# One kernel for a whole transformer layer: no ada rows in the last value group of the first input projection, and 1.06 rows per unit in the first output projection

## The chip, the cores and the metric

The kernel runs on one core of one Trainium2 chip. The metric is the device time of one execution in microseconds (us); for the kernel before the change three runs are given.

## What is computed

One layer over 256 tokens of width 2048, in float32: a first SwiGLU block of inner width 5632, a token mixer (forget-gate attention and an mLSTM), and a second SwiGLU block. Each block takes a layer norm of the running activation, shifted and scaled by values computed from a condition vector `c`, and each block's result is gated by further values of the same kind before it is added back.

```python
def _modulate(x, shift, scale):
    return _layernorm(x) * (1 + scale) + shift

def _swiglu(h, w_in, w_out):
    gate, up = jnp.split(h @ w_in, 2, axis=-1)
    return (jax.nn.silu(gate) * up) @ w_out

...
    ada = (jax.nn.silu(c) @ w_ada + b_ada)[:, None, :]
    sh1, sc1, g1, sh2, sc2, g2, sh3, sc3, g3 = jnp.split(ada, N_ADA, axis=-1)
    h = _swiglu(_modulate(x, sh1, sc1), ffn1_w_in, ffn1_w_out)
    x = _layernorm(ALPHA * x + 0.5 * (1 + g1) * h, ln1_g, ln1_b)
    h = _token_mixer(_modulate(x, sh2, sc2), w_in, fox_f_bias, mlstm_conv_w, mlstm_conv_b,
                     mlstm_i_bias, mlstm_f_bias, mlstm_norm_g, w_out)
    x = _layernorm(ALPHA * x + (1 + g2) * h, ln2_g, ln2_b)
    h = _swiglu(_modulate(x, sh3, sc3), ffn2_w_in, ffn2_w_out)
    x = _layernorm(ALPHA * x + 0.5 * (1 + g3) * h, ln3_g, ln3_b)
```

The product of `c` with `w_ada` (2048 by 18432) is the "ada" work. The change touches only when parts of it are done.

## The kernel before

**Matrix products.** Every large product is made of three TensorE matmuls on split operands: a float32 matrix is split into a rounded part `hi` (a cast on ScalarE, L155) and a remainder `lo` (a subtraction on VectorE, L156), and `hi*hi`, `hi*lo` and `lo*hi` are added up in PSUM (L435 to L437). Weights come by DMA on SyncE's queue into `raw` tiles of 1 MB (three of them), are split in two halves of 128x1024 into `hi` and `lo` tiles (six of each), and are used once. One `raw` tile is called a unit here.

**The first SwiGLU block.** `ffn_in` multiplies by `ffn1_w_in`. Its loop takes 256 inner features at a time, first the gate columns (`gu` = 0) and then the up columns (`gu` = 1, the value group); two PSUM tiles `gu_f` hold both. At the end of each turn ScalarE takes the silu of the gate half into `hT` (L474) and VectorE multiplies it by the up half (L475). `out_proj` then multiplies `hT` by `ffn1_w_out` in columns of 1024, 512 and 512. Its first four PSUM tiles, `o_f`, come from the same rotation of five as `gu_f`: with two tiles held by the last turn, the fourth `o_f` tile is one of those two, and is free when its L475 is done. On L156's tiles the two stages are called `f1i` and `f1o`.

**The ada rows.** A row of ada work is a DMA of 512 KB of `w_ada` into a tile `ar` (two of them, tag `araw`, L188 and L189) and one multiply-and-add on VectorE into an accumulator `acc` (L170). Sixteen rows make one accumulator of the queue; then a tail splits it and sums it over partitions on TensorE (`bc`, L183), with a few small VectorE steps (`dg`, `scsh`, L200 to L204). The rows are handed out along the way by a queue object: after each half unit, and after each unit, the stage's rate is credited and whole rows that are owed are written into the program.

```python
        def half_step(self):
            n = self.rate / 2
            self.given += n
            self.owed += n
            self.owed_rows()

        def pump(self, n):
            self.owed += n - self.given
            self.rate, self.given = n, 0
            self.end_step()
            self.owed_rows()

        def rest(self):
            self.owed = self.rate = self.given = 0
```

The rates stand in one line (L814): 1.2 rows per unit in the first input projection (`R_IN`), 1 in the first output projection (`R_OUT`). `out_proj` pumps after 40 of its 44 units: the last four get tails alone. Before it ends, at `need(6)`, the four accumulators for the mixer's shift and scale (`acc3_0` to `acc3_3`, shown as `acc_0` to `acc_3`) must be complete; the boundary to the mixer reads them.

**What sets the order.** Dependencies are tracked by the framework, which also orders each engine's instructions from the written program; VectorE, ScalarE and SyncE then run their lists strictly in that order.

Of the kernel before, what the change touches and what calls it, by code (L numbers as in the profile page):

```python
# [32 lines left out]
def layer_kernel(  # L33
# [35 lines left out]
    def mm_tile(name, four=False):  # L69
        turn[0] = 0 if four else turn[0] % 5 + 1  # L70
        if turn[0] == 5:
            return fifth_tile(name)
        return pm.tile([P, 512], F32, tag="mm", bufs=4, name=name)
# [218 lines left out]
    ada = AdaQueue()  # L292
# [134 lines left out]
    def unwoven(ps):  # L427
        return ps.rearrange("p (n a) -> p a n", a=2)

    def halves(v):  # L430
        return v.rearrange("p (a n) -> p a n", a=2)

    def mm3(o, ah, al, bh, bl, start, stop):
        bh, bl = woven(bh), woven(bl)
        PE.matmul(o, ah, bh, start=start, stop=False)  # L435
        PE.matmul(o, ah, bl, start=False, stop=False)  # L436
        PE.matmul(o, al, bh, start=False, stop=stop)  # L437

    def mm2(o, ah, al, x, start, stop):
        PE.matmul(o, ah, x.rearrange("p s (a n) -> p s n a", a=2), start=start, stop=False)  # L440
        PE.matmul(o[:, T:], al, woven(x[:, 0]), start=False, stop=stop)  # L441


    def cols_form_a(src, c0, outs, xT, name, npump, khs=(0, 1)):
        xhi, xlo, x = xT
        for kh in khs:
            for k8, hi, lo in load_w(src[kh * 1024:(kh + 1) * 1024, c0:c0 + 256], 8, 256, f"{name}_{kh}"):
                k = kh * 8 + k8
                for f in range(2):
                    fs = slice(f * P, (f + 1) * P)  # L450
                    start, stop = k == 8 * khs[0], k == 8 * khs[-1] + 7
                    if outs[f].shape[-1] == 2 * T:
                        mm2(outs[f], hi[:, fs], lo[:, fs], x[:, k], start, stop)
                    else:
                        mm3(outs[f], hi[:, fs], lo[:, fs], xhi[:, k, :], xlo[:, k, :], start, stop)
            npump()

    def ffn_in(w, xT, hT, j0, tag, npump, values=None):
        def one(j, gu, outs):
            last = gu and j == DFF // 256 - 1  # L460
            cols_form_a(w, gu * DFF + j * 256, outs, xT, f"{tag}i{j}_{gu}", (lambda: None) if last else npump)

        def both(dst, ps):
            S.copy(dst, unwoven(ps[:, :T]))
            V.tensor_tensor(out=dst, in0=dst, in1=unwoven(ps[:, T:]), op=ALU.add)

        for j in range(j0, DFF // 256):
            if values is None:
                ps = [mm_tile(f"gu_{tag}{j}_{f}") for f in range(2)]
                for gu in range(2):  # L470
                    one(j, gu, [p[:, gu * T:(gu + 1) * T] for p in ps])
                for f in range(2):
                    h = halves(hT[:, 2 * j + f, :])
                    S.activation(h, unwoven(ps[f][:, :T]), AF.Silu)  # L474
                    pin["h"] = V.tensor_tensor(out=h, in0=h, in1=unwoven(ps[f][:, T:]), op=ALU.mult).ins  # L475
                continue
            for gu in range(2):
                ps = [mm_tile(f"gu_{tag}{j}_{gu}{f}") for f in range(2)]
                one(j, gu, ps)
                for f in range(2):  # L480
                    h = halves(hT[:, 2 * j + f, :])
                    if gu:
                        u = halves(values.tile([P, T], F32, tag="u", bufs=2, name=f"u_{tag}{j}_{f}"))
                        both(u, ps[f])
                        pin["h"] = V.tensor_tensor(out=h, in0=h, in1=u, op=ALU.mult).ins
                    else:
                        both(h, ps[f])
                        S.activation(h, h, AF.Silu)
        for _ in range(2):
            npump()  # L490


# [312 lines left out]
    def entry_of(load, got, u0, u1):  # L805
        for u in range(u0, u1):
            got[u] = []
            for item in load(u):
                got[u].append(item)
                yield  # L810

    R_F, R_IN, R_OUT, R_MX, R_A, R_B = 1.25, 1.2, 1, 1.26, 1, .7  # L814
    NP = 2
    right = dict(side="right")
    def at(rate):
# [255 lines left out]

    first_hi_places("1")
    ffn_in(W1, xT, hT, NS, "f1", at(R_IN))
    xp.release()
    need(2)
# [62 lines left out]
    fence, _, xs, ws = boundary(*ent["f"], ent["lgb"], 3, "1", xT, entry_of(mo_load, mow, 3, 6), KD, raws)  # L1140
# [14 lines left out]
    xhi, xlo, _ = xT  # L1155
# [522 lines left out]
    for us in (0, 1), (2,):  # L1678
        for q in QS:
            last = q == QS[-1]  # L1680
# [27 lines left out]
    h_parts.clear()  # L1708
    vals = tc.alloc_tile_pool(name="vals2", bufs=1)
    ffn_in(W2, xT, hT, 2 + NH, "f2", at(R_B), vals)  # L1710
    vals.release()
    need(14)
# [42 lines left out]
```

## Time and profile before

| what | us |
|---|---|
| three runs | 1862.06, 1863.48 (median), 1869.91 |
| the profiled execution, its own time | 1865.56 |
| its span in the profile | 1863.9 |
| TensorE matmuls busy in it | 1830.1 |
| VectorE busy | 1455.8 |
| ScalarE busy | 913.5 |

The times are of whole executions; the profile is of one more execution, and the sum in the prediction is made against that one's own time, 1865.56 us. In the rows that follow, PE is TensorE's matmuls, PEld its weight loads, DVE VectorE, ACT ScalarE, SPq SyncE's DMA queue. Times in timelines are counted from the start of the span. A row of a timeline gives the start, the duration of the (merged) instructions, the engine, the line, the operation, what it writes and reads, and, in brackets, how long the engine had been idle and what released it.

### The profile page before, as it was taken

To read this page: it belongs to the slowest core of one execution; us is meant where nothing else is said; L and a number is where in the kernel's file an instruction comes from. 1 tells how busy PE (TensorE), PEld (TensorE's weight loads), DVE (VectorE), ACT (ScalarE), POOL (GpSimd) and SP (SyncE) were. 2 spreads that over 40 slices of the span, in tenths; PEclk is the share of its full clock that TensorE was granted. 3 is DMA by queue.
4 is the path that set the end of the run, shared out by engine and by line. 5 is a ranking of instruction groups with operands and counts; after the bars stand their busy time and mean duration, and the time that the engine had idled before them with its cause. 6 is when DMAs were issued, how large, how long until landed. Compare 5 with 4: busy or idle time off the path is not lost.

```text
span 1863.9 us, 30963 instructions
## 1 busy us (share of the span) xinstructions
PE 1830.1 (98%) x12521; PEld 1694.2 (91%) x12521; DVE 1455.8 (78%) x1819; ACT 913.5 (49%) x1290; POOL 62.1 (3%) x92
## 2 busy tenths in 40 slices
PE   7999999999999999999999999999999999999997
PEld 5999999999988888689999887999999999988887
DVE  6889989778788787778889878777998776574655
ACT  3554454443454434655566645545454444554441
POOL 1211200000000000000000000000000000000000
PEclk9999999999999999999999999999999999999999
DMA  9989978999897889389978883998878876666663
GB/s 366 383 278 316 319 236 283 321 322 318 285 324 273 311 296 326 129 283 330 313 275 293 324 290 131 343 324 271 293 255 275 273 251 201 198 202 204 204 203 144
DMA packets 263431, 510.82 MB, mean 274 GB/s; under 512 B 10834, under 2 KB 93426, under 8 KB 262264
## 3 DMA queue, kind: packets, MB, share of 16 engines
q1 hardware_dynamic: 255176, 477.90, 74.9%
q0 software_dynamic: 8112, 30.95, 4.8%
q8 instruction: 98, 1.61, 0.4%
q14 instruction: 45, 0.37, 0.1%
HBM read 506.71 MB, written 2.10 MB: 273 GB/s over the span
## 4 chain that ended last, share of the span: by engine, by line
PE 56%; DVE 2%; DMA 1%; issue 1%; ACT 0%; POOL 0%; DVEq 0%; ACTq 0%; POOLq 0%
PE gu_f L440 8%; PE o_f L435 4%; PE o_f L437 4%; PE o_f L436 4%; PE fh L435 4%; PE fh L437 4%; PE fh L436 4%; PE gu_f L441 4%; PE o_mx L435 1%; PE o_mx L436 1%; PE o_mx L437 1%; PE b_mv L435 1%; PE pr_m L435 1%; PE b_mv L436 1%; PE b_mv L437 1%; PE pr_m L437 1%
## 5 line engine op out<-in xcount | busy, mean ns | idle before, releaser
L170 DVE SCALAR_TENSOR_TENSOR acc<-ar,csil,acc 128x1024 f32<-128x1024 f32 (+1 forms) x167 | 211.8, 1269 | 65.7 <-DMA ar<-in_w_ada_dram 65.1
L435 PE MATMUL s<-x_f,hi_s 128*128 128x256 f32 x768 | 211.7, 276 | 1.3 <-DVE hT L1014 1.1
L437 PE MATMUL s<-x_f,lo_s 128*128 128x256 f32 x768 | 211.3, 275 | 0.9 <-DVE lo_s L156 0.7
L436 PE MATMUL s<-x_f,hi_s 128*128 128x256 f32 x768 | 211.4, 275 | 0.0
L440 PE MATMUL gu_f<-x_f,hi_f2i 128*128 128x512 f32 x640 | 209.9, 382 | 0.0
L435 PE MATMUL fh<-x_f,hi_fh 128*128 128x256 f32 x640 | 176.2, 275 | 0.0
L437 PE MATMUL gu_f<-x_f,lo_f1i 128*128 128x256 f32 x640 | 176.0, 275 | 0.0
L437 PE MATMUL fh<-x_f,lo_fh 128*128 128x256 f32 x640 | 176.0, 275 | 0.0
L436 PE MATMUL gu_f<-x_f,hi_f1i 128*128 128x256 f32 x640 | 176.0, 275 | 0.0
L436 PE MATMUL fh<-x_f,hi_fh 128*128 128x256 f32 x640 | 176.0, 275 | 0.0
L435 PE MATMUL gu_f<-x_f,hi_f1i 128*128 128x256 f32 x640 | 176.0, 275 | 0.0
L441 PE MATMUL gu_f<-x_f,lo_f2i 128*128 128x256 f32 x640 | 174.4, 273 | 0.0
L156 DVE TENSOR_TENSOR lo_f2o<-raw_f2o,hi_f2o 128x1024 fp32r<-128x1024 f32 x86 | 105.3, 1225 | 86.7 <-ACT hi_f2o L155 86.6
L155 ACT CAST hi_s<-raw_s 128x1024 fp32r<-128x1024 f32 x96 | 99.5, 1051 | 127.7 <-PE s L436 80.0
L155 ACT CAST hi_f1o<-raw_f1o 128x1024 fp32r<-128x1024 f32 x86 | 89.3, 1048 | 122.0 <-PE o_f L437 73.7
L435 PEld LDWEIGHTS s<-x_f,hi_s 128*128 128x128 f32 x768 | 147.3, 192 | 1.6 <-DVE hT L1014 1.3
L437 PEld LDWEIGHTS s<-x_f,lo_s 128*128 128x128 f32 x768 | 147.4, 192 | 1.2 <-DVE lo_s L156 1.2
L436 PEld LDWEIGHTS s<-x_f,hi_s 128*128 128x128 f32 x768 | 147.4, 192 | 0.4 <-DVE x_f L352 0.4
L155 ACT CAST hi_f2o<-raw_f2o 128x1024 fp32r<-128x1024 f32 x86 | 90.0, 1047 | 115.6 <-PE o_f L437 111.2
L156 DVE TENSOR_TENSOR lo_f2i<-raw_f2i,hi_f2i 128x1024 fp32r<-128x1024 f32 x80 | 97.9, 1224 | 49.2 <-ACT hi_f2i L155 48.6
L440 PEld LDWEIGHTS gu_f<-x_f,hi_f2i 128*128 128x128 f32 x640 | 121.0, 189 | 16.9
L435 PE MATMUL o_f<-hi_f1o,hi 128*128 128x512 f32 x344 | 131.8, 383 | 3.3 <-DVE hT L475 3.3
(444 smaller groups left out, 5254.1 us busy)
## 6 DMA issues: line engine op xcount, KB each, us to landing
ar<-in_w_ada_dram SPq DMA_DIRECT2D x230, 512.0 KB, 5.6
raw_s<-in_ffn_w_in_dram SPq DMA_DIRECT2D x47, 1024.0 KB, 7.4
raw_f1o<-in_ffn_w_out_dram SPq DMA_DIRECT2D x44, 1024.0 KB, 7.3
raw_f2o<-in_ffn_w_out_dram SPq DMA_DIRECT2D x44, 1024.0 KB, 5.2
raw_f1i<-in_ffn_w_in_dram SPq DMA_DIRECT2D x40, 1024.0 KB, 7.7
raw_fh<-in_ffn_w_in_dram SPq DMA_DIRECT2D x40, 1024.0 KB, 6.5
raw_f2i<-in_ffn_w_in_dram SPq DMA_DIRECT2D x40, 1024.0 KB, 5.1
ar<-in_w_ada_dram POOLq DMA_DIRECT2D x45, 512.0 KB, 6.8
```

Of the source, the lines that this page charges most:

```text
L155: S.copy(hi, src)
L156: return V.tensor_tensor(out=lo, in0=src, in1=hi.bitcast(F32), op=ALU.subtract)
L170: V.scalar_tensor_tensor(out=acc, in0=raw, scalar=csil[:, k:k + 1], in1=acc, op0=ALU.mult, op1=ALU.add)
L435: PE.matmul(o, ah, bh, start=start, stop=False)
L436: PE.matmul(o, ah, bl, start=False, stop=False)
L437: PE.matmul(o, al, bh, start=False, stop=stop)
L440: PE.matmul(o, ah, x.rearrange("p s (a n) -> p s n a", a=2), start=start, stop=False)
L441: PE.matmul(o[:, T:], al, woven(x[:, 0]), start=False, stop=stop)
```

## The change

```diff
     def ffn_in(w, xT, hT, j0, tag, npump, values=None):
         def one(j, gu, outs):
             last = gu and j == DFF // 256 - 1
+            if last and tag == "f1":
+                ada.rest()
             cols_form_a(w, gu * DFF + j * 256, outs, xT, f"{tag}i{j}_{gu}", (lambda: None) if last else npump)
...
-        for _ in range(2):
+        for _ in range(2 * (tag != "f1")):
             npump()
...
-    R_F, R_IN, R_OUT, R_MX, R_A, R_B = 1.25, 1.2, 1, 1.26, 1, .7
+    R_F, R_IN, R_OUT, R_MX, R_A, R_B = 1.25, 1.2, 1.06, 1.26, 1, .7
```

In the last value group of the first input projection the rate is set to zero, so the half steps inside `load_w` hand out no row, and the two pumps after the loop are left out for this stage. The first output projection gets 1.06 rows per unit in place of 1. No instruction is added or removed on any engine; on VectorE, ScalarE, TensorE (tails) and SyncE some change places.

The first place is VectorE's list at the end of the first input projection. `hT_129` with `gu_f_0` is the last turn's multiply whose PSUM tile the output projection's fourth tile takes over; `lo_f1o_11` is the `lo` of unit 1, half 1 of the output projection. Before:

```order
L170 SCALAR_TENSOR_TENSOR acc_1_5977<-ar_1_7_6093,csil,acc_1_5977 128x1024
L156 TENSOR_TENSOR lo_f1o_01_6306<-raw_f1o_0_6287,hi_f1o_01_6305 128x1024
L156 TENSOR_TENSOR lo_f1o_10_6330<-raw_f1o_1_6327,hi_f1o_10_6329 128x1024
L170 SCALAR_TENSOR_TENSOR acc_1_5977<-ar_1_8_6154,csil,acc_1_5977 128x1024
L170 SCALAR_TENSOR_TENSOR acc_1_5977<-ar_1_9_6215,csil,acc_1_5977 128x1024
L156 TENSOR_TENSOR lo_f1o_11_6346<-raw_f1o_1_6327,hi_f1o_11_6345 128x1024
L156 TENSOR_TENSOR lo_f1o_20_6370<-raw_f1o_2_6367,hi_f1o_20_6369 128x1024
L475 TENSOR_TENSOR hT_129<-hT_129,gu_f_0_6000 128x256
L156 TENSOR_TENSOR lo_f1o_21_6386<-raw_f1o_2_6367,hi_f1o_21_6385 128x1024
L475 TENSOR_TENSOR hT_129<-hT_129,gu_f_1_6001 128x256
L170 SCALAR_TENSOR_TENSOR acc_1_5977<-ar_1_10_6250,csil,acc_1_5977 128x1024
```

The same place in the changed kernel (its lines are two higher from there on):

```order
L170 SCALAR_TENSOR_TENSOR acc_1_5977<-ar_1_7_6093,csil,acc_1_5977 128x1024
L156 TENSOR_TENSOR lo_f1o_01_6297<-raw_f1o_0_6278,hi_f1o_01_6296 128x1024
L156 TENSOR_TENSOR lo_f1o_10_6321<-raw_f1o_1_6318,hi_f1o_10_6320 128x1024
L156 TENSOR_TENSOR lo_f1o_11_6337<-raw_f1o_1_6318,hi_f1o_11_6336 128x1024
L156 TENSOR_TENSOR lo_f1o_20_6361<-raw_f1o_2_6358,hi_f1o_20_6360 128x1024
L477 TENSOR_TENSOR hT_129<-hT_129,gu_f_0_6000 128x256
L156 TENSOR_TENSOR lo_f1o_21_6377<-raw_f1o_2_6358,hi_f1o_21_6376 128x1024
L477 TENSOR_TENSOR hT_129<-hT_129,gu_f_1_6001 128x256
L170 SCALAR_TENSOR_TENSOR acc_1_5977<-ar_1_8_6312,csil,acc_1_5977 128x1024
```

Rows 8 and 9 of `acc_1` moved from ahead of the two multiplies to behind them; rows 6 and 7 still stand ahead; rows 10 and 11, which stood just behind, follow later.

The second place is SyncE's DMA queue, a little later: weights of the output projection (`raw_f1o`, 1 MB each) and rows (`ar`, 512 KB each). Before:

```order
L396 DMA raw_f1o_2_6367<-in_ffn_w_out_dram 128x2x1024
L189 DMA ar_1_8_6154<-in_w_ada_dram 128x2x512
L189 DMA ar_1_9_6215<-in_w_ada_dram 128x2x512
L396 DMA raw_f1o_3_6407<-in_ffn_w_out_dram 128x2x1024
L189 DMA ar_1_10_6250<-in_w_ada_dram 128x2x512
L189 DMA ar_1_11_6321<-in_w_ada_dram 128x2x512
L396 DMA raw_f1o_4_6447<-in_ffn_w_out_dram 128x2x1024
L396 DMA raw_f1o_5_6487<-in_ffn_w_out_dram 128x2x1024
```

The same queue in the changed kernel:

```order
L396 DMA raw_f1o_2_6358<-in_ffn_w_out_dram 128x2x1024
L189 DMA ar_1_8_6312<-in_w_ada_dram 128x2x512
L189 DMA ar_1_9_6352<-in_w_ada_dram 128x2x512
L396 DMA raw_f1o_3_6398<-in_ffn_w_out_dram 128x2x1024
L396 DMA raw_f1o_4_6438<-in_ffn_w_out_dram 128x2x1024
L396 DMA raw_f1o_5_6478<-in_ffn_w_out_dram 128x2x1024
L189 DMA ar_1_10_6392<-in_w_ada_dram 128x2x512
L189 DMA ar_1_11_6432<-in_w_ada_dram 128x2x512
```

The DMAs of rows 8 and 9 keep their place; those of rows 10 and 11 moved behind the weights of units 4 and 5.

The third place is VectorE's list near the end of the output projection, in its last 512 columns: the last two rows of `acc_3`, and `alo_3_0`, the first step of its tail. Before:

```order
L170 SCALAR_TENSOR_TENSOR acc_3_7352<-ar_3_14_7745,csil,acc_3_7352 128x1024
L156 TENSOR_TENSOR lo_f1o_30_7751<-raw_f1o_3_7748,hi_f1o_30_7750 128x1024
L156 TENSOR_TENSOR lo_f1o_31_7767<-raw_f1o_3_7748,hi_f1o_31_7766 128x1024
L170 SCALAR_TENSOR_TENSOR acc_3_7352<-ar_3_15_7782,csil,acc_3_7352 128x1024
L156 TENSOR_TENSOR lo_f1o_40_7788<-raw_f1o_4_7785,hi_f1o_40_7787 128x1024
L156 TENSOR_TENSOR lo_f1o_41_7804<-raw_f1o_4_7785,hi_f1o_41_7803 128x1024
L156 TENSOR_TENSOR alo_3_0_7820<-acc_3_7352,ahi_3_0_7819 128x512
```

The same place in the changed kernel:

```order
L170 SCALAR_TENSOR_TENSOR acc_3_7422<-ar_3_14_7779,csil,acc_3_7422 128x1024
L156 TENSOR_TENSOR lo_f1o_40_7785<-raw_f1o_4_7782,hi_f1o_40_7784 128x1024
L156 TENSOR_TENSOR lo_f1o_41_7801<-raw_f1o_4_7782,hi_f1o_41_7800 128x1024
L170 SCALAR_TENSOR_TENSOR acc_3_7422<-ar_3_15_7816,csil,acc_3_7422 128x1024
L156 TENSOR_TENSOR lo_f1o_50_7822<-raw_f1o_5_7819,hi_f1o_50_7821 128x1024
L156 TENSOR_TENSOR lo_f1o_51_7838<-raw_f1o_5_7819,hi_f1o_51_7837 128x1024
L156 TENSOR_TENSOR alo_3_0_7854<-acc_3_7422,ahi_3_0_7853 128x512
```

The third accumulator ends one unit later than before, still inside the units in which rows are handed out.

## The prediction

> **What bounds the kernel now.** I read the page first, for the engine that is never free, then the waits of that engine, then the stretch in which its only wait that the change can touch lies. On the page the first row is the span, the second gives busy time, share and count of each engine, and the last is a group of matmuls with its idle time and what ended it.
>
> ```profile
> span 1863.9 us, 30963 instructions
> PE 1830.1 (98%) x12521; PEld 1694.2 (91%) x12521; DVE 1455.8 (78%) x1819; ACT 913.5 (49%) x1290; POOL 62.1 (3%) x92
> ...
> L435 PE MATMUL o_f<-hi_f1o,hi 128*128 128x512 f32 x344 | 131.8, 383 | 3.3 <-DVE hT L475 3.3
> ```
>
> TensorE's matmuls are busy for 1830.1 of 1863.9 us. The change adds and removes no matmul, so it can only act on TensorE's 33.8 us of idle time, on its clock, or on new waits. The waits of TensorE (total, times, longest) name where the idle time lies.
>
> ```profile
> PE row L924 <- DMA hT<-in_w_ada_dram: 7.1, 3, 6.6
> PE o_f L435 <- DVE hT L475: 3.3, 1, 3.3
> ...
> PE b_fv L436 <- DVE lo_fv L156: 1.5, 1, 1.5
> ```
>
> The largest, 6.6 us, is in the opening, which the change leaves alone. The second is one wait of 3.3 us: the first output projection waits for VectorE's multiply L475, and that multiply is where the change works. The table by stretches shows what else happens there; after the window come its length, busy time of PE, PEld, DVE, ACT and POOL, then the granted TensorE clock, the DMA share and GB/s.
>
> ```profile
> 529.00:535.00 6.00, 6.00 (x15) 4.79 (x16) 6.00 (x7) 2.60 (x4) 0.00 (x0) 0.51 1.01 377
> 535.00:547.00 12.00, 12.00 (x57) 10.52 (x56) 9.71 (x11) 10.74 (x16) 0.00 (x0) 1.00 0.89 317
> ...
> 600.00:640.00 40.00, 40.00 (x187) 35.01 (x187) 30.79 (x27) 15.73 (x16) 0.00 (x0) 1.00 0.97 347
> 690.00:742.00 52.00, 52.00 (x242) 45.26 (x241) 40.11 (x41) 23.18 (x24) 1.06 (x2) 1.00 0.90 315
> 790.00:1100.00 310.00, 308.23 (x2209) 291.50 (x2210) 261.56 (x394) 185.05 (x343) 6.68 (x10) 1.00 0.88 303
> ```
>
> For 6 us behind the wait the clock was 0.51, and then 1.00 again. So the wait has a second price, which the busy time hides. From 535 to 742, to near the end of the projection, TensorE has no gap at all in the rows shown. In the stretch that holds the 1.5 us wait (`b_fv`, 790 to 1100) the clock stayed 1.00: a short wait does not bring this price.
>
> **The wait and the slow clock, priced.** TensorE's timeline around it:
>
> ```profile
> 523.56 0.38 PE L435 MATMUL o_f<-hi_f1o,hi 128*128 128x512 f32 x1
> ...
> 525.29 0.38 PE L437 MATMUL o_f<-hi_f1o,lo 128*128 128x512 f32 x1
> 529.00 0.79 PE L435 MATMUL o_f<-hi_f1o,hi 128*128 128x512 f32 x1 [3.33 <-DVE hT L475]
> ...
> 533.42 0.63 PE L436 MATMUL o_f<-lo_f1o,hi 128*128 128x512 f32 x1
> 533.85 0.63 PE L437 MATMUL o_f<-hi_f1o,lo 128*128 128x512 f32 x1
> ...
> 534.99 0.38 PE L437 MATMUL o_f<-hi_f1o,lo 128*128 128x512 f32 x1
> ```
>
> Nine matmuls start from 523.56 to 525.29, eight steps of 0.216 us. The tenth, the first into the fourth PSUM tile, would start at 525.51 and starts at 529.00: 3.49 us lost. From 529.00 to 534.99 are 14 steps (the stretch counts 15 starts), 5.99 us, where 14 times 0.216 would be 3.03: another 2.96 us lost, at 0.43 us a matmul. Together the place costs 6.45 us.
>
> The Trainium skill, "TensorE: Matmul & The Clock Gate", Part 1 on the HAM clock gate, gives 426.7 ns as the cold step of a 512-column matmul; the steps of 0.43 here agree. The same section says that the clock halves after an idle window of about 3.4 us and that these windows run free. A wait of 3.49 us need then not trip it in every execution; this is a rival below.
>
> **Why VectorE is late, and what the change does to it.** VectorE's rows up to the multiply, and ScalarE's casts and silu that feed them:
>
> ```profile
> 517.73 2.61 DVE L170 SCALAR_TENSOR_TENSOR acc<-ar,csil,acc 128x1024 f32<-128x1024 f32 x2 [2.41 <-DMA ar<-in_w_ada_dram]
> 520.26 2.35 DVE L156 TENSOR_TENSOR lo_f1o<-raw_f1o,hi_f1o 128x1024 fp32r<-128x1024 f32 x2
> 523.21 1.28 DVE L170 SCALAR_TENSOR_TENSOR acc<-ar,csil,acc 128x1024 f32<-128x1024 f32 x1 [0.59 <-DMA ar<-in_w_ada_dram]
> 525.06 1.28 DVE L170 SCALAR_TENSOR_TENSOR acc<-ar,csil,acc 128x1024 f32<-128x1024 f32 x1 [0.57 <-DMA ar<-in_w_ada_dram]
> 526.26 2.35 DVE L156 TENSOR_TENSOR lo_f1o<-raw_f1o,hi_f1o 128x1024 fp32r<-128x1024 f32 x2
> 528.53 0.42 DVE L475 TENSOR_TENSOR hT<-hT,gu_f 128x256 f32<-128x256 f32 x1
> ```
>
> ```profile
> 518.33 1.05 ACT L155 CAST hi_f1o<-raw_f1o 128x1024 fp32r<-128x1024 f32 x1 [1.51 <-PE gu_f L436]
> 521.59 1.05 ACT L155 CAST hi_f1o<-raw_f1o 128x1024 fp32r<-128x1024 f32 x1 [2.21 <-DMA raw_f1o<-in_ffn_w_out_dram]
> 523.43 0.38 ACT L474 ACTIVATE hT<-gu_f 128x256 f32<-128x256 f32 x1 [0.79 <-PE gu_f L437]
> ```
>
> The rows at 517.73 are ada rows 6 and 7, those at 523.21 and 525.06 rows 8 and 9, each waiting for its DMA. Rows 8 and 9 take VectorE from the end of the second `lo` (two of them take 2.35 us, so 1.13 us a step: 520.26 + 2.27 = 522.53) to 526.26: 3.73 us. They go behind the multiply. The two next `lo` then start at 522.53 and 523.66; their casts end at 519.38 and 522.64, in time. The multiply starts at 524.80 instead of 528.53; its silu ended at 523.81, so it does not wait for that. It takes 0.42 us and ends at 525.22. The tenth matmul wants it at 525.51. The margin is 0.29 us, so the whole wait goes and the slow clock with it: minus 6.45 us.
>
> What this margin rests on: rows 6 and 7 still stand ahead, and they waited 2.41 us for their DMA. Their DMAs and that of unit 2's weights (ScalarE waited 2.21 us for it) keep their place in SyncE's queue and nothing ahead of them moves, so I take their times as they are. If a DMA lands later than here by more than 0.29 us, the wait returns by the excess. The bounds for this term are thus minus 6.45 and, with VectorE as late as now, 0; nearest to what the order says is the full 6.45.
>
> The two trailing pumps held rows 10 and 11. They were behind the multiply already, so leaving them out frees nothing on the path; their two DMAs (512 KB each) move behind the weights of units 4 and 5, which are issued sooner. On SyncE the queue issues in order, and unit 4's weights no longer wait behind rows that need a free `ar` tile. I price this at zero because TensorE has no gap in the rows of the stretches from 535 on.
>
> **What the output projection takes on.** Two rows (8 and 9) are new work behind the multiply: 2.5 us on VectorE (523.21 to 526.26, less the idle 0.57), 1 MB on the DMA queues. The rate of 1.06 over 40 units hands out 42.4 rows where 40 are left of the three accumulators (8 of `acc_1`, 16 of `acc_2`, 16 of `acc_3`), so nothing is forced at `need(6)`; the order shows the tails of TensorE at the end in their old places. The cover is the lead with which weights are split ahead of use. VectorE's and TensorE's timelines show it near the end of the projection, where it is short:
>
> ```profile
> 726.36 1.29 DVE L406 TENSOR_TENSOR dlo<-raw_f1o,dhi 128x512 fp32r<-128x512 f32 x2 [5.41 <-ACT dhi L403]
> ...
> 729.91 3.49 DVE L156 TENSOR_TENSOR lo_f1o<-raw_f1o,hi_f1o 128x1024 fp32r<-128x1024 f32 x3
> ```
>
> ```profile
> 739.11 0.40 PE L183 MATMUL bc<-ahi,trir 128*128 128x512 f32 x1
> ```
>
> From 524 to 765, ScalarE's casts of these weights waited as follows (total, times, longest):
>
> ```profile
> ACT hi_f1o L155 <- PE o_f L437: 73.7, 48, 3.9
> ACT hi_f1o L155 <- DMA raw_f1o<-in_ffn_w_out_dram: 35.0, 13, 5.3
> ```
>
> The first of the three `lo` at 729.91 is the second half of unit 6 in the last columns and ends at 731.1. TensorE uses it in the 12 matmuls before 739.11, from about 736.5: a lead of 5.4 us. After the change TensorE comes there 6.45 us sooner, VectorE's list 3.73 us sooner, and 2.5 us of rows are added ahead: the lead falls by at most 5.2, to 0.2. That is the worst case, in which none of VectorE's idle time in between gives way; the 690 to 742 stretch alone has 11.9 us of it, and the last two rows (ScalarE held back 48 times by TensorE, which has yet to free a tile, and 13 times by weights) say that the lead is refilled to what the buffers allow more often than it runs out. So I take zero for this term and keep a gain lost in whole as its other bound.
>
> The boundary to the mixer and all behind it start sooner by the same amount and are in the same order on every engine.
>
> **Sum.** 1865.56 (the profiled execution) minus 6.45 is 1859.1. Against the median of the runs, 1863.48, which is 2.1 below the profiled execution, it is 1857.0. I cannot say whether those 2.1 us are a slow clock that some runs do not have, or the profiling; I take the middle, 1858.0.
>
> **The rivals.**
> A wait that stays in part: the margin is only 0.29 us and two DMAs decide it. Half of the wait, 1.7 us, would leave 1859.8, and up to 1862.7 if the clock halved again (2.96). For it: both DMAs are late now. Against: nothing ahead of them moves.
> The slow clock is a matter of phase: if most of the timed runs before have the 3.49 us wait at full clock, the change takes 3.49 from the median, 1860.0. For it: the median lies 2.1 below the profiled execution. Against: the one execution that is seen had it. By the page's free-running windows this would differ from run to run.
> A shortage of weights in the output projection, in the bursts of rows: it decides for slower once TensorE loses more than 6.45 us there. One wait like today's, 3.49 with 2.96 of slow clock, gives all back: 1863.5. Two of them make it 1869.9. For it: a lead that may fall to 0.2, DMA shares of 0.97 and 0.90 in the rows above, a higher rate. Against: 11.9 us of slack in the last stretch.
> More than 6.45 is hard to find: the 1.5 us wait and the boundaries are not touched. If the profiled stall is longer in the timed runs, 1854 could come out.
>
> **How the numbers follow.** Chances: 0.56 for the full gain (1858.0, from 1855.6, which is 1857.0 less the 1.4 us between median and lowest run, to 1860); 0.13 for a wait that stays in part; 0.15 for the matter of phase; 0.10 for the shortage; 0.06 for more than the sum. About 0.5%, 9.3 us, is what a measurement of this kernel can tell from no change: faster by that is below 1854.2, slower above 1872.8. Faster takes the 0.06 of the last case, slower half of the shortage, 0.05, since it needs three such waits or a steady lack; all else, 0.89, is within. The range goes from 1855.5 to 1863.5, the time with nothing gained, and leaves out the last case and most of the shortage.
>
> **What would show it.** In the profile after: the wait of `o_f` for `hT` gone or below 1 us; the clock 1.00 between 520 and 540; matmul steps of 0.216 there; the first matmul of the boundary about 6 us sooner, and so all later landmarks. Wrong would show as TensorE waits for `lo_f1o` or `dlo` between 535 and 760, as a second slow stretch of the clock, or as an execution before that has no slow stretch at all.

## The result and the profile after

Against 17 runs of the kernel before (median 1864.86 us), 17 runs of the changed kernel have a median of 1871.4 us (1865.27 to 1891.9): the ratio is 1.0037, 95% interval [1.0021, 1.0053]. The change made the kernel slower by about 0.4%; the forecast was 1858.0 us with a range that ended at 1863.5. The profiled execution took 1875.11 us.

The page of the changed kernel, its span and its TensorE row:

```profile
span 1873.4 us, 30958 instructions
PE 1832.9 (98%) x12521; PEld 1697.3 (91%) x12521; DVE 1455.9 (78%) x1819; ACT 914.4 (49%) x1290; POOL 62.2 (3%) x92
```

The matmul count is the same. TensorE's waits after (total, times, longest):

```profile
PE bc L183 <- ACT ahi L155: 7.9, 1, 7.9
PE row L926 <- DMA hT<-in_w_ada_dram: 7.0, 3, 6.6
PE o_f L435 <- DVE res L557: 3.1, 1, 3.1
```

The wait for `hT` that the prediction priced is gone. Two others have come that the profile before did not show. The table by stretches has the clock at the old place and at the two new ones (the column of 1.00 or 0.50 is the granted clock):

```profile
524.00:530.00 6.00, 6.00 (x29) 5.25 (x29) 5.47 (x7) 4.31 (x8) 0.00 (x0) 1.00 0.96 348
640.60:647.40 6.80, 6.11 (x15) 4.89 (x16) 6.80 (x10) 1.05 (x1) 0.00 (x0) 0.50 0.73 250
743.00:753.00 10.00, 5.25 (x12) 4.15 (x13) 4.83 (x6) 2.51 (x3) 0.00 (x0) 0.50 0.78 273
```

At 524 the step is gone and the clock is full, as forecast. At 640 and 743 each new wait has a slow clock behind it. TensorE's timeline at these two places:

```profile
637.86 0.38 PE L437 MATMUL o_f<-hi_f1o,lo 128*128 128x512 f32 x1
641.29 0.77 PE L435 MATMUL o_f<-hi_f1o,hi 128*128 128x512 f32 x1 [3.05 <-DVE res L557]
...
647.38 0.38 PE L437 MATMUL o_f<-hi_f1o,lo 128*128 128x512 f32 x1
...
739.44 0.38 PE L437 MATMUL o_f<-dhi,lo 128*128 128x512 f32 x1
747.75 0.79 PE L183 MATMUL bc<-ahi,trir 128*128 128x512 f32 x1 [7.93 <-ACT ahi L155]
...
753.31 0.38 PE L437 MATMUL o_f<-hi_f1o,lo 128*128 128x512 f32 x1
```

With the step of 0.216 us of the prediction: at 637.86 the next start was due at 638.08 and came at 641.29, 3.21 lost; 14 steps to 647.38 took 6.09 where 3.02 were due, 3.07 lost; together 6.28. At 739.44 the next was due at 739.66 and came at 747.75, 8.09 lost; 13 steps to 753.31 took 5.56 where 2.81 were due, 2.75 lost; together 10.84. The balance of the two profiles is minus 6.45 plus 6.28 plus 10.84, which is 10.7; the two executions differ by 9.55.

**The first place, at the change of width.** The first 1024 columns end at 637.86, and the next columns need a PSUM tile back, for which VectorE must gate and add the old one (L555, L557). VectorE's rows after:

```profile
634.38 1.28 DVE L170 SCALAR_TENSOR_TENSOR acc<-ar,csil,acc 128x1024 f32<-128x1024 f32 x1
...
639.26 0.69 DVE L555 TENSOR_TENSOR o_f<-o_f,gate 128x512 f32<-128x512 f32 x1
639.87 0.68 DVE L156 TENSOR_TENSOR alo<-acc,ahi 128x512 fp32r<-128x512 f32 x1
640.47 0.68 DVE L557 SCALAR_TENSOR_TENSOR res<-res,o_f 128x512 f32<-128x512 f32 x1
```

The last row of the second accumulator (634.38, the one before it at 630.90), and the first step of its tail (`alo`) between the two instructions that free the PSUM tile, have come here. This is work that the change put off. In the kernel before, VectorE waits for ScalarE's casts of the weights here and has nothing of ada in its list:

```profile
641.09 1.23 DVE L156 TENSOR_TENSOR lo_f1o<-raw_f1o,hi_f1o 128x1024 fp32r<-128x1024 f32 x1 [1.37 <-ACT hi_f1o L155]
```

**The second place, at the end of the projection.** `bc` of the last accumulator's second half needs `ahi`, a cast on ScalarE. ScalarE's rows after:

```profile
745.18 1.99 ACT L155 CAST hi_f1o<-raw_f1o 128x1024 fp32r<-128x1024 f32 x2 [5.69 <-DMA raw_f1o<-in_ffn_w_out_dram]
747.08 0.61 ACT L155 CAST ahi<-acc 128x512 fp32r<-128x512 f32 x1
```

The cast of `ahi` needs only the accumulator, but it stands in ScalarE's list behind the two casts of unit 10, the last weights, and they waited 5.69 us for their DMA. The same place before, first ScalarE's timeline and then TensorE's:

```profile
737.95 1.04 ACT L155 CAST hi_f1o<-raw_f1o 128x1024 fp32r<-128x1024 f32 x1 [0.71 <-DMA raw_f1o<-in_ffn_w_out_dram]
739.31 1.06 ACT L155 CAST hi_f1o<-raw_f1o 128x1024 fp32r<-128x1024 f32 x1 [0.31 <-PE o_f L437]
740.26 0.61 ACT L155 CAST ahi<-acc 128x512 fp32r<-128x512 f32 x1
```

```profile
740.93 0.50 PE L183 MATMUL bc<-ahi,trir 128*128 128x512 f32 x1
```

The order was the same, and `ahi` ended at 740.87 for a `bc` that started at 740.93. There was no slack at all: `bc` was in time by 0.06 us, because unit 10 was there 7.2 us earlier (737.95 against 745.18). What else the DMA engines carry at that time is seen in two views. In the table by stretches DMA share and GB/s are the last two columns; the first is of before, the second of after. The third is SyncE's timeline after and the fourth GpSimd's, with the start and duration of each issue.

```profile
725.00:735.00 10.00, 10.00 (x48) 8.75 (x47) 7.04 (x8) 5.88 (x6) 0.57 (x2) 1.00 0.51 180
735.00:744.00 9.00, 8.72 (x40) 7.02 (x39) 6.63 (x8) 4.60 (x5) 0.49 (x1) 1.00 1.03 403
```

```profile
725.00:735.00 10.00, 10.00 (x48) 8.77 (x47) 7.27 (x9) 4.94 (x5) 1.06 (x2) 1.00 0.85 287
735.00:744.00 9.00, 4.82 (x23) 3.84 (x21) 2.68 (x3) 1.99 (x2) 0.00 (x0) 0.94 1.03 402
```

```profile
725.22 1.41 SPq L189 DMA_DIRECT2D ar<-in_w_ada_dram  x1
730.11 0.97 SPq L396 DMA_DIRECT2D raw_f1o<-in_ffn_w_out_dram  x2
```

```profile
733.21 0.54 POOL L614 DMA_DIRECT2D lg<-in_ln_g_dram  x1 [311.83 <-ACT hi_f1o L155]
```

Before, the DMA engines were half idle from 725 to 735; the last ada row was long in. After, they carry rows and weights at 0.85, and from 735 on they are full in both kernels. The row load at 725.22 is none of the projection's own: VectorE adds the projection's last row at 720.62 and its next row only at 810.13. It is a row of the next accumulator, fetched as soon as a row tile is free, and it stands in SyncE's list ahead of the weights of units 9 and 10 (the two issues at 730.11); in the kernel before, the last row load went out at 714.79. The layer norm's parameters `lg` and `lb`, two loads of 1 MB on GpSimd's queue, 0.5 us apart, that are released by the progress of the projection itself, then share the engines with unit 10: at 402 GB/s their 2 MB are 5.2 us, an estimate.

**Six executions.** One profile before and one after are one execution each. Two further profiled executions of each kernel were taken, with these expectations.

> The kernel before, unchanged, profiled once more. If the wait of o_f for hT is the same in every execution, it is 3 to 3.6 us again, with a slow clock of 6.8 us behind it, and the gain I forecast was there to be had. If it hangs on when the rows' DMAs land, it lies anywhere between 0.5 and 3.5 us, and the slow clock is missing in some executions.

> As the run before it in this list: 3 to 3.6 us with a slow clock if the wait is the same in every execution; between 0.5 and 3.5 us, at times without a slow clock, if it hangs on the rows' DMAs.

> The changed kernel, unchanged, profiled once more. If the meeting of lg and lb with the last weights is the rule, bc waits 6 us or more for ahi again and the weights of unit 10 land 10 us or more after their issue; if the first profile showed a rare case, the wait is below 3 us. The wait at the change of width: 2 to 3.5 us by the reading of the first profile.

> As the run before it in this list: bc waits 6 us or more and the wait at the change of width is 2 to 3.5 us, if both are the rule in the changed kernel.

Start of the first matmul of each stage, in us; "last columns" are the 512 columns that begin the last turn of products (`dhi`), "mixer" its first `mo`:

| | before, first profile | again | again | after, first profile | again | again |
|---|---|---|---|---|---|---|
| output projection | 523.6 | 522.2 | 523.6 | 522.5 | 527.4 | 522.8 |
| `dhi` | 739.6 | 734.9 | 735.4 | 738.4 | 739.1 | 740.3 |
| `mo` | 763.4 | 766.8 | 758.8 | 772.3 | 771.3 | 770.4 |
| execution | 1865.56 | 1867.68 | 1860.46 | 1875.11 | 1874.54 | 1872.05 |

The mean difference of the executions is 9.3 us. It lies 1.1 ahead of the projection (made by the one execution at 527.4, which has two slow stretches of the clock in the opening), 1.5 from there to `dhi`, 5.7 from `dhi` to `mo` (26.4 us before, 32.1 after), and 1.0 behind. The gain at the start is given back before 740, and the loss is made in the last 25 us of the projection. The waits of the two repeats before, two rows of the first and one of the second, and then of the two after:

```profile
PE bc L183 <- ACT ahi L155: 5.6, 1, 5.6
PE o_f L435 <- DVE hT L475: 2.9, 1, 2.9
```

```profile
PE o_f L435 <- DVE hT L475: 1.9, 1, 1.9
```

```profile
PE bc L183 <- ACT ahi L155: 6.1, 1, 6.1
...
PE o_f L435 <- DVE res L557: 1.9, 1, 1.9
```

```profile
PE bc L183 <- ACT ahi L155: 4.4, 1, 4.4
...
PE o_f L435 <- DVE res L557: 2.1, 1, 2.1
```

Two things were hidden in a single profile. The kernel before has the wait at the tail too, in one of three executions; after, it is in all three. In that one execution before, `lg` was issued 0.6 us behind unit 10, and unit 10 took 10.2 us from its issue to its cast; in the other two `lg` came 2.9 and 4.6 us behind, and unit 10 took 6.4 and 6.9. After, it took 14.1, 12.3 and 11.8. And the wait for `hT` was 3.3, 2.9 and 1.9 us before, with a slow clock behind it in the first execution alone.

### The profile page after: what moved, and what is told of

It reads as the page before. It is cut to its first block, busy times and chain, and to the rows that moved or that the text cites. A ratio compares the mean times of both kernels' runs of the same rounds, so it can differ in the third digit from the quotient of the medians.

```text
span 1873.4 us, 30958 instructions
## 1 busy us (share of the span) xinstructions
PE 1832.9 (98%) x12521; PEld 1697.3 (91%) x12521; DVE 1455.9 (78%) x1819; ACT 914.4 (49%) x1290; POOL 62.2 (3%) x92
## 4 chain that ended last, share of the span: by engine, by line
PE 54%; DVE 3%; DMA 1%; issue 1%; ACT 0%; POOL 0%; DVEq 0%; ACTq 0%; POOLq 0%
PE gu_f L440 7%; PE o_f L435 4%; PE o_f L436 4%; PE o_f L437 4%; PE fh L436 4%; PE fh L435 4%; PE fh L437 4%; PE gu_f L441 4%; PE o_mx L437 1%; PE o_mx L436 1%; PE o_mx L435 1%; PE b_mv L435 1%; PE b_fv L435 1%; PE b_mv L436 1%; PE b_fv L436 1%
## 5 line engine op out<-in xcount | busy, mean ns | idle before, releaser
L170 DVE SCALAR_TENSOR_TENSOR gate<-ar,csil,gate 128x1024 f32<-128x1024 f32 (+1 forms) x94 | 117.6, 1252 | 25.5 <-DMA ar<-in_w_ada_dram 24.9
```

Of the source, the lines that this page charges most:

```text
L170: V.scalar_tensor_tensor(out=acc, in0=raw, scalar=csil[:, k:k + 1], in1=acc, op0=ALU.mult, op1=ALU.add)
```

## The experiments

Two theories stood against each other at first: that the higher rate starves the projection of weights (the prediction's own rival), and that rows put off meet two places without slack, one at the change of width and one at the tail.

**The rate, and the rest, alone.** The changed kernel with the rate of before, and the kernel before with the rate of the change:

```diff
-    R_F, R_IN, R_OUT, R_MX, R_A, R_B = 1.25, 1.2, 1.06, 1.26, 1, .7
+    R_F, R_IN, R_OUT, R_MX, R_A, R_B = 1.25, 1.2, 1, 1.26, 1, .7
```

> The change with the rate of the first output projection left at 1.0 (the rows of the last value group and of the two pumps go, and nothing makes them up). Tail theory: the changed kernel loses because the last tail matmul of acc3_3 waits for a ScalarE cast that stands behind the casts of the last weights (unit 10); here that cast stands in the same place, so the wait of bc for ahi stays, 4 to 8 us with a slow clock behind it, and the time is 1868 to 1874. Supply theory: the rate of 1.06 starves the weights; without it the loss goes and the gain of 6.4 us stays, 1857 to 1862.

> The kernel before with 1.06 rows per unit in the first output projection and nothing else. Both theories: the wait of o_f for hT stays (3.3 us with the slow clock). Tail theory: the tail of acc3_3 comes one unit sooner and its last cast stands ahead of the casts of units 9 and 10, so no wait of bc above 1 us and a time equal to before, 1862 to 1867. Supply theory: more rows per unit starve the weights, TensorE waits for lo_f1o or for the add-up between 535 and 760, 1868 to 1872.

The rest without the rate: 1869.9 us, ratio 1.0028 [1.0013, 1.0043], and the wait of `bc` for `ahi` is there in full, 8.0 us, with 1.8 at the change of width. The rate without the rest: 1866.46 us, 1.0007 [0.9985, 1.0029], without these two waits; its one profile has two short waits for `lo_f1o` instead (2.2 us together, at 755 to 758). So putting the rows off is enough for the loss, and the rate alone shows none, though its interval leaves room for some. Which part of the rest does it, the rate of zero in the last value group or the two pumps left out, was not separated.

**The rows made up earlier, or faster.** The changed kernel with 1.3 rows per unit in the input projection in place of 1.2 and 1 in the output projection; and with 1.2 rows per unit in the output projection:

```diff
-    R_F, R_IN, R_OUT, R_MX, R_A, R_B = 1.25, 1.2, 1.06, 1.26, 1, .7
+    R_F, R_IN, R_OUT, R_MX, R_A, R_B = 1.25, 1.3, 1, 1.26, 1, .7    # rows earlier
+    R_F, R_IN, R_OUT, R_MX, R_A, R_B = 1.25, 1.2, 1.2, 1.26, 1, .7  # rate 1.2
```

> The change with the missing rows made up in the first input projection (1.3 rows per unit there in place of 1.2) and 1.0 in the output projection. Tail theory: the tail of acc3_3 comes a unit sooner, its last cast stands behind the casts of unit 9 and ahead of those of unit 10; the wait of o_f for hT is gone, the wait of bc falls to 0 to 4 us, and 1858 to 1864 comes out. Supply theory: no more rows in the output projection than before, so the whole gain shows, 1857 to 1860.

> The change with 1.2 rows per unit in the first output projection in place of 1.06. Tail theory: the tail of acc3_3 ends in the units before the last four, its casts stand ahead of those of unit 7, the wait of bc (8.1 us and 2.8 us of slow clock) goes: 1858 to 1864, with the wait at the change of width (3.2 and 3.1 us) perhaps left. Supply theory: still more rows per unit starve the weights more than 1.06 does: 1873 to 1880.

Earlier rows: 1862.75 us, 0.9993 [0.9974, 1.0013], with neither new wait in its profile, and the loss is gone. Rate 1.2: 1870.0 us, 1.0033 [1.0013, 1.0054]. There the tail ends earlier and `bc` does not wait for `ahi`, but the wait at the change of width stays at 3.5 us, and waits for weights (`hi_f1o` 1.6, `lo_f1o` 1.5) stand near 746 to 750. The profiled execution took 1867.58 us, less than the median; what the other runs lose is not seen.

**The slow clock at the old place, filled.** The kernel before, with 26 matmuls of 256 columns into a scratch tile, whose result nothing reads, in the gap where TensorE waits for `hT`:

```diff
+                        if tag == "f1" and col + k == 0 and a and b:
+                            scratch = aux_tile("fill")
+                            for _ in range(26):
+                                PE.matmul(scratch[:, :T], onesr, trir, start=True, stop=True)
```

> The kernel before with 26 matmuls of 256 columns, into a spare PSUM tile that nothing reads, between the ninth and tenth matmul of the first output projection, where TensorE waits for hT: they add no wait (2.9 us of work in a gap of 3.5 us) and keep TensorE busy. If the slow clock behind the wait is caused by the gap, the clock stays 1.00 there and the stretch of 14 matmuls takes 3.0 us instead of 6.0; if the whole gain were kept the time would be 1862 (minus 2.9). Rival: the end of the projection is set by the landing of the last weights, so TensorE only waits longer for bc near 740 and the time stays 1864 to 1866.

It took 1862.46 us, 1.0007 [0.9987, 1.0026]: no slow clock in the profile, and no gain in the runs. This fits a slow clock that the runs before mostly did not have.

**The layer norm's loads held back.** Two runs put the issue of `lg` and `lb` later in the written order only. In the first the loads were still issued at 733.24 and 733.77 us, in the second at 727.38 and 727.91, so nothing was held, and the two stand as repeats of the changed kernel and of the one with rows earlier.

> The changed kernel with the two loads of the layer norm's parameters (lg and lb, 1 MB each) held on GpSimd's queue until the second split of unit 9 in the last columns. Collision theory: in the changed kernel these loads start 2.6 us after the last weights' (unit 10) and these land after 14 us, against 3.5 us and 6.4 us before; held back, unit 10 lands in 6 to 7 us, the wait of bc for ahi falls from 7.9 us to 0 to 2 us with no slow clock, and the time falls by 6 to 11 us against the changed kernel, to 1861 to 1866 (the wait at the change of width stays). Tail theory without a collision: the cast stands behind the last weights whatever GpSimd loads, the wait stays above 5 us, 1868 to 1873. A third way, that the loads are then late for the boundary: TensorE's first mo matmul is no sooner than in the changed kernel though bc no longer waits.

> The change with its rows made up in the first input projection (1.3 there, 1.0 in the output projection) and with lg and lb held until the second split of unit 9. Collision theory: lg and lb came 4.2 us behind unit 10 in the same kernel without the hold, which did no harm, so the hold is worth little: 1859 to 1863, within 2 us of the kernel without the hold (1862.75). Rival: the parameters are then late for the boundary, 1864 to 1867.

They gave 1872.93 us, 1.0056 [1.0038, 1.0074] (6 runs), and 1861.78 us, 0.9998 [0.9986, 1.0010]. A hold that works has VectorE write one column of each tile behind the first split of unit 9, so that the loads wait for it:

```diff
+                    if tag == "f1" and lastg and i == nu - 2 and kk == 1:
+                        ent["load"](lo)
...
+            def load(lo):
+                for t, src in zip(lgb, (g, b)):
+                    V.tensor_scalar_add(t[:, 0:1], lo[:, 0:1].bitcast(F32), EPS)
+                    G_.dma_start(t, src.to_broadcast([P, D]))
...
```

> The changed kernel with the loads of lg and lb truly held: VectorE writes one column of each from the first split of unit 9 (two operations of 128x1), so that GpSimd's loads wait for it; the earlier attempt to hold them only set an order and left them at 733.8 us. Collision theory: unit 10 lands 6 to 8 us after its issue, not 14; the wait of bc for ahi falls from 7.9 us to 0 to 2 us, the wait at the change of width stays, and the time falls by 5 to 10 us against the changed kernel, to 1861 to 1866. Tail theory without a collision: unit 10 lands late in any case, the wait stays above 5 us, 1868 to 1873. Third way: the parameters come late for the boundary and TensorE's first mo matmul is no sooner than in the changed kernel.

> The kernel before with the true hold alone. Collision theory: before, lg and lb start to move only when unit 10 has landed, so the hold is worth nothing: within 0.2% of before, unit 10 lands 6 to 7 us after its issue. Rival: held loads are late for the boundary and cost 2 to 4 us.

> The change with its rows made up in the first input projection (1.3 there, 1.0 in the output projection), with the true hold. If the rows of the output projection and the meeting of the loads are all that stood against the change, its gain shows here: 1857 to 1861, 3 to 6 us below before. If the gain is only the slow clock in some executions: 1860 to 1863, within 0.15% of before.

On the changed kernel: 1867.84 us, 1.0015 [0.9996, 1.0034]. Its wait at the tail:

```profile
PE bc L183 <- ACT ahi L155: 3.0, 1, 3.0
```

The wait at the tail is 3.0 us, less than in any of the four profiles of that order without the hold (7.9, 6.1, 4.4, 9.4), and the weights of unit 10 needed 9.3 us from issue to cast where they needed 11.8 to 14.1 in the three profiles of the changed kernel. The interval overlaps that of the changed kernel, so these runs alone do not show the gain; the profile does, for one execution. On the kernel before (1862.7 us, 0.9992 [0.9974, 1.0009]) and on the one with rows earlier (1862.3 us, 0.9994 [0.9977, 1.0011]) the hold changes nothing that can be measured. In the profile of the former the wait for `hT` is 0.8 us, at full clock.

**A pause at the change of width.** 1.2 rows per unit, but none in the last four units of the first 1024 columns; and the same with the hold:

```diff
-                if lastg and i >= nu - 4:
+                quiet = (lastg or tag == "f1" and col == 0) and i >= nu - 4
+                if quiet:
                     ada.rest()
...
-                if not lastg or i < nu - 4:
+                if not quiet:
                     npump()
...
```

> The change with 1.2 rows per unit in the output projection and no rows in the last four units of its first 1024 columns. With 1.2 alone TensorE waited 3.5 us at the change of width for VectorE's add-up (res), which stands on VectorE behind rows and splits. If rows are what makes VectorE late there, the wait falls to below 1 us; if it is the landing of the weights, it stays at 3 us or more. The time then: 1865 to 1868 if only this wait goes (1870.0 with 1.2 alone), since the last weights still meet lg and lb.

> The kernel with 1.2 rows per unit and no rows in the last four units of the first 1024 columns, with the true hold of lg and lb in addition. The pause took the wait at the change of width away and left 6.3 us at bc. Collision theory: with the hold bc waits at most 2 us, so all three waits (hT, width, bc) are gone, and the time is 1858 to 1863, 5 us or more below the pause alone (1868.4). Rival: the last weights are late because of the rows alone, and the wait stays above 4 us, 1866 to 1869.

The pause alone: 1868.39 us, 1.0028 [1.0016, 1.0039]. The wait at the change of width is gone, the one at the tail is 6.3 us. With the hold: 1863.35 us, 0.9990 [0.9972, 1.0007], and 2.3 us at the tail. These two intervals do not meet, so here the runs do show what the hold is worth: without it `lg` is issued at 726.61 and unit 10 needs 9.5 us from issue to cast, with it at 736.38 and 4.8 us. The width's wait is thus made by rows near it, and taking it away alone does not make up the loss.

**The queue behind unit 10's cast.** The last step moves the cast: both halves of the last accumulator are split at the place of the first half, the second into a row tile that is free by then. The second half's subtraction on VectorE and its two matmuls on TensorE come forward with it.

```diff
+    def early_split(acc, tag):
+        p = ap.tile([P, 2, 512], F32R, tag="araw", bufs=2, name=f"ahl{tag}")
+        split(acc, p[:, 0], p[:, 1])
+        return p[:, 0], p[:, 1]
...
-            parts = ada_split(acc[:, i, :], f"{v}_{j}_{i}")
+            if (v, j) == (3, 3):
+                if i == 0:
+                    early = [ada_split(acc[:, 0, :], "3_3_0"), early_split(acc[:, 1, :], "3_3_1")]
+                parts = early[i]
+            else:
+                parts = ada_split(acc[:, i, :], f"{v}_{j}_{i}")
```

> The changed kernel, with one thing more: both halves of the last accumulator of the output projection are split at the place of the first half (the second half into a free row tile), so that the last cast of that tail no longer stands behind the cast of unit 10's weights on ScalarE. No load is moved. Theory (the queue behind unit 10's cast makes the wait at the tail): TensorE has no wait of bc for ahi near 740 even where unit 10 lands as late as in the changed kernel, and 6 to 10 us of its time go: about 1863, ratio 0.996 to 1.001. Rival (unit 10's late landing itself holds TensorE): the wait returns some us later as a wait for hi_f1o or lo_f1o before 765, and the time stays at 1868 to 1872.

> The same, and the pause at the change of width as in the run with a pause (1.2 rows per unit in the output projection, none in the last four units of the first 1024 columns). Theory (the two waits together are all that the change loses): neither the wait of o_f for res near 640 nor the one of bc for ahi near 745; what is left is the gain at the start of the projection, 2 to 6 us: 1857 to 1861, ratio 0.997 to 0.999. Rival (the DMA queues have no room for the rows that come later, so some other wait for weights stands for them): 1863 or more, with waits for weights between 640 and 765.

The first: 1864.25 us, 0.9996 [0.9974, 1.0018], where the changed kernel has 1.0037 [1.0021, 1.0053]; the two intervals do not meet. TensorE's, ScalarE's and SyncE's timelines (`ahl` is the second half):

```profile
736.29 0.63 PE L188 MATMUL bc<-ahl,trir 128*128 128x512 f32 x2
```

```profile
739.74 1.99 ACT L155 CAST hi_f1o<-raw_f1o 128x1024 fp32r<-128x1024 f32 x2 [3.84 <-DMA raw_f1o<-in_ffn_w_out_dram]
```

```profile
737.79 0.46 SPq L194 DMA_DIRECT2D ar<-in_w_ada_dram  x1
```

Unit 10 is late here too: its casts end at 741.73. In the old order `ahi` would have followed them and ended at 742.34, some 4.7 us after TensorE would have asked for it, six matmuls behind the first half's `bc` (an estimate). Now `bc` runs at 736.29 without a wait, and no wait for weights takes its place; the wait at the change of width is still there, 1.7 us. But this run does not move the cast alone, and "No load is moved" does not hold. The row tile that the split takes holds back a load: the row that the changed kernel loads at 725.22, ahead of units 9 and 10, goes out at 737.79, behind them, and unit 10 takes 9.9 us from issue to cast where it took 11.8 to 14.1. So the 7.2 us between the medians (1871.4 and 1864.25) belong to the place of the cast and to that load together.

With the pause as well: 1861.15 us, 0.9974 [0.9954, 0.9993]. Set beside the pause alone (1868.39 us, 1.0028 [1.0016, 1.0039]) this is the cleaner proof: from 690 us to the mixer SyncE issues the same loads in the same order in both, both row loads of the next accumulator behind unit 10. First the pause alone, ScalarE and TensorE, then the pause with the split moved:

```profile
736.98 1.99 ACT L155 CAST hi_f1o<-raw_f1o 128x1024 fp32r<-128x1024 f32 x2 [6.17 <-DMA raw_f1o<-in_ffn_w_out_dram]
```

```profile
739.54 0.80 PE L183 MATMUL bc<-ahi,trir 128*128 128x512 f32 x1 [6.31 <-ACT ahi L155]
```

```profile
738.88 1.99 ACT L155 CAST hi_f1o<-raw_f1o 128x1024 fp32r<-128x1024 f32 x2 [5.16 <-DMA raw_f1o<-in_ffn_w_out_dram]
```

```profile
731.50 0.63 PE L188 MATMUL bc<-ahl,trir 128*128 128x512 f32 x2
```

Unit 10 is about as late in both, 9.5 and 8.8 us from issue to cast. The wait of 6.3 us is gone; the ratios are 0.0054 apart, some 10 us, and their intervals lie clear of each other. So at the tail the late weights cost TensorE time through the place of one cast of 0.61 us, with the subtraction and the two matmuls that hang on it.

The rival, that late weights hold TensorE by themselves, is left with little: 0.9 us in two waits for `lo_f1o` near 741 to 743 in this profile. For weights that come later still it has a share. In the run at rate 1.2, where `bc` did not wait, unit 10 was cast at 745.30, about as late as in the first profile after (745.18), and TensorE waited 3.1 us for `hi_f1o` and `lo_f1o`.

The pause with the split moved is the only version that beats the kernel before, by about 0.3% or 3.7 us of the medians; its interval ends close to 1, and it is one of fourteen versions timed. The stretches at the two places that the change brought into play, the start of the projection and the change of width, are without a gap and at full clock:

```profile
520.00:545.00 25.00, 25.00 (x126) 22.16 (x126) 21.98 (x24) 19.24 (x30) 0.00 (x0) 1.00 0.90 315
630.00:650.00 20.00, 20.00 (x94) 17.52 (x93) 18.47 (x23) 8.53 (x9) 0.00 (x0) 1.00 0.85 301
```

That it is faster than the version without the pause is likely but not shown, since their intervals overlap.

## Why the prediction was wrong

- **The local step was right.** "So the whole wait goes and the slow clock with it": the wait is gone in all three profiles after, and 524 to 530 runs at full clock.
- **Its size was wrong.** The 6.45 us came from one execution. With waits of 3.3, 2.9 and 1.9 us and a slow clock in one of three, the mean is 2.7 us, plus a third of the 2.96 us, about 3.7. The rival on the phase of the clock, at 0.15, described this; the sign that was named for it, "an execution before that has no slow stretch at all", came twice in the repeats at this place.
- **The step that failed is the cover of the output projection.** "So I take zero for this term" rested on a lead of 5.4 us, read at unit 6's `lo` on VectorE. The cover that failed was ScalarE's list: the instruction with the least slack stood some microseconds later and on another engine: `bc` for `ahi`, 0.06 us. "The order shows the tails of TensorE at the end in their old places" was true and proved nothing, since a place in a list says what an instruction stands behind, not when that arrives. The profile before had the row (`ahi` at 740.26 behind unit 10's cast), and it wasn't read.
- **"The boundary to the mixer and all behind it start sooner by the same amount" failed.** `mo` starts 8.3 us later in the mean of three. The prediction left two kinds of loads out: `lg` and `lb` on GpSimd's queue, which run into the last weights (2.1, 2.1 and 3.4 us behind unit 10's issue in the three profiles after), and the next accumulator's row, which is fetched ahead of units 9 and 10 once the projection's rows end a unit later.
- **The second place was missed.** The rows were priced as 2.5 us of VectorE beside a lead of weights. What waited was not weights but PSUM: the gate and the add that free a tile at the change of width stand in the same list behind the rows. TensorE waited 1.9 to 3.1 us there, with a slow clock in two of three. What this costs the runs is not shown by itself: the intervals with and without that wait overlap.
- **The signs were partly right.** "A second slow stretch of the clock" was named as what wrong would look like, and came. "TensorE waits for `lo_f1o` or `dlo`" was the wrong instruction: except for one of 1.9 us in a repeat, the waits are for `res` and for `ahi`. The shortage rival was priced right (1869.9 for two waits) and given the wrong mechanism: at the old rate the loss stays (1.0028), and with the pause in both, moving the one cast takes 1.0028 to 0.9974.
- **What stays open.** Why unit 10 lands late has two parts. That `lg` and `lb` are one is shown by the pause with and without the hold. How much the row loads add is not: the split moved without the pause shifts one of them, and the cast with it. Why "rows earlier" gains, by its ratios, no more than 0.07% (0.9993, 0.9998 and 0.9994 in its three versions), although both new waits are gone and the old one is down to 1.0 us or less, is open too: the rows moved into the input projection may cost there what they save. In its three profiles the output projection begins at 525.9, 523.0 and 529.1 us, against 522.5, 527.4 and 522.8 in the changed kernel, which is too spread to tell.

## What to carry to other kernels

Before work is put off to a later stage, look in that stage for the instruction with the least slack on every engine that works in list order, small casts and PSUM-freeing adds included; the lead of the big stream says nothing about them. A short instruction whose input is ready belongs ahead of an instruction that waits for a DMA, not behind it. And a wait that is read in one execution should be read in two or three before its whole length, and the slow clock behind it, is booked as a gain.

## What the runs showed of the hardware

The slow clock does not follow the length of the wait. In the run at rate 1.2, TensorE waits for 3.50 us and the stretch around it stays at full clock; in a repeat of the changed kernel, waits of 2.1 and 1.9 us (`res` at the change of width and `lo_f1o` at 712) are each followed by a slow stretch. First the timeline and the stretch of the run at rate 1.2, then two stretches of the repeat:

```profile
642.12 0.45 PE L435 MATMUL o_f<-hi_f1o,hi 128*128 128x512 f32 x1 [3.50 <-DVE res L557]
```

```profile
636.00:646.00 10.00, 6.50 (x31) 5.40 (x30) 9.73 (x13) 5.14 (x6) 0.00 (x0) 1.00 1.03 385
```

```profile
641.70:645.10 3.40, 3.40 (x10) 2.68 (x9) 3.40 (x6) 1.05 (x1) 0.00 (x0) 0.50 0.93 343
713.40:716.80 3.40, 3.40 (x10) 2.68 (x9) 3.40 (x4) 1.99 (x2) 0.00 (x0) 0.51 0.71 240
```

Away from the two ends of the span, the slow stretches were 3.4, 6.8 or 10.2 us long in these profiles, multiples of 3.4. The Trainium skill, "TensorE: Matmul & The Clock Gate", Part 1 on the HAM clock gate, has free-running windows of about 3.4 us; the lengths agree with that. It asks for an idle window of that length before the clock halves; the 2.1 and 1.9 us waits here did it without one, so by this trace a partly idle window can be enough. The prediction's "a short wait does not bring this price" held for the 1.5 us that it looked at, and not for these.

GpSimd's loads slow SyncE's: in the version with the pause, with the DMA engines at 0.99 of their time from 725 to 735, two 1 MB loads on GpSimd's queue and the last 1 MB of weights on SyncE's queue were in flight together, and the weights took 9.5 us from issue to cast. With the GpSimd loads held until the weights were in, at 0.96, they took 4.8 us. The Trainium skill, "DMA: Bandwidth & Descriptors", section "Issuing engines are not separate DMA queues", says that transfers of all issuing engines run on the same 16 DMA engines and interleave; these rows agree.
